# A decoder layer's opening: memory turned raw, memory weights ahead of x, half of x turned among the queries, and the mLSTM pools laid out anew

## The chip, the core and the metric

The kernel runs on one core of a Trainium2 chip. Work is spread over the core's engines, each with its own instruction queue: TensorE (PE, matmuls and transposes, with its weight loads shown as PEld), VectorE (DVE), ScalarE (ACT), GpSimd (POOL), and SyncE (SP), which issues the transfers between HBM and the on-chip memory SBUF. The metric is device microseconds of one execution. The kernel before took 2228.19 us (median of three runs, 2226.64 to 2229.35).

## The reference

One layer over 1024 tokens of width 1024, in float32. What the change touches is the head of the layer and the memory branch, branch C:

```
h = rms_norm(x, norm_mix_g)
proj = h @ w_in                      # the last 512 columns of it are cq
mkv = rms_norm(mem, mem_g) @ w_kv    # 256 memory tokens; 512 key + 1024 value columns
mk = rms_norm(mk per head of 128, k_g);  qh = rms_norm(cq per head of 128, q_g)
p = softmax(qh @ mk.T * 128 ** -0.5);    y_c = p @ mv
gates = sigmoid(h @ w_gate + b_gate)     # 3 x 1024 columns
```

After it come the mLSTM branch, differential attention, three output projections merged by the gates, and an MLP with residuals. The row norm multiplies each row of `mem` by one factor, so it commutes with the matrix product: `(r * mem) @ w = r * (mem @ w)`.

## The kernel before, in words

**Split products.** Every float32 operand of a product is split into a high part (rounded to the matmul type) and a low rest, and a product is three matmuls: high x high, high x low, low x high (`mm3`). A split (`split`, L107) is one ACT instruction for the high part and one DVE instruction for the low part; the low part needs the high part. Operands that must be turned go through a PE transpose into PSUM first; four 128x128 blocks share one PSUM tile, and the splits read it from there. The pool for these tiles, `tp`, has two buffers.

**The opening, `phase_x` with `mem_kv`.** All in one queue order on each engine: two memory tiles (128 tokens x 1024) and the first weights are loaded; each memory tile is squared and summed on ACT (L231), the factor `r` is worked out on POOL (L127, L128), and DVE multiplies the tile by it (L233); then PE turns it (L243) and ACT and DVE split it into `memT` (L114, L115). The key weights `wkv[0]` are loaded in four pieces of 512 KB through a pool of three raw buffers (`rp`) and split (L111, L112). Keys of two token tiles are made one after the other, normed, turned and split into `mkT`. Then the eight tiles of x are loaded; four are normed and turned into the first half of `hT` (`half(0)`), the values from `wkv[1]` follow, `half(1)` does the second half of x, and the values from `wkv[2]` end it. `hT` is the turned, split, normed x that everything later multiplies with.

**Branch C, `branch_c`.** A `stream` of eight query tiles (24 matmuls each, yielding after every three: a position) and then 64 gate positions; `weave` puts other items at positions written out by hand: turn a query tile (`turn`, at 8t + 12), its scores and softmax (`scores`, at 8t + 15, with four exponentials on ACT, L380), the turning of the probabilities (`ptr`) and the products with the values. PE runs this order as written (`pinned`). ACT, DVE, POOL and SP instructions are not pinned: a planner orders them for each engine by readiness and program order, at build time. [...]

**Gates.** `gate_load` loads and splits gate weights in pieces of 256 columns, `gate_steps` runs the gate products; the first two gate groups run at the end of branch C, and each result `gt` is stored through SP (L472).

**The mLSTM branch, `branch_m`.** It begins with eight value tiles `v_tile(3, t)` of 24 matmuls of 264 columns (`wmv`), for which eight weight pieces are loaded into `rp` (three raw buffers) and split into `wp` (25 buffers). Pools are laid out one after the other from the same start as branch C's pools. Before: `gm` (value tiles, gate vectors), `pm3`, `rp`, `wp`, so that the 25 weight buffers lie over what branch C still holds; a buffer can be written once everything that lay on its bytes has been read.

```
gm, pm3, self.rp, self.wp = E2("gm", 1), E2("pm3", 3), E2("rpm", 3), E2("wpm", 25)
```

Of the kernel before, what the change touches and what calls it, by code (L numbers as in the profile page):

```python
# [10 lines left out]
F32 = mybir.dt.float32  # L11
F32R = mybir.dt.float32r
AF = mybir.ActivationFunctionType
# [4 lines left out]
P = 128  # L18
D = 1024
S = 1024  # L20
NT = 8
# [10 lines left out]
def f32(ap):  # L32
    return ap.bitcast(F32)
# [38 lines left out]
class Layer:  # L72
    def __init__(self, tc, a, out):
        self.tc, self.nc, self.a, self.out = tc, tc.nc, a, out
        self.V, self.A = InOrder(tc, tc.nc.vector), tc.nc.scalar
        self.n = 0

# [29 lines left out]
    def split(self, hi, lo, src, scale=None):  # L107

        nc = self.nc
        if scale is None:  # L110
            nc.scalar.copy(hi, src)  # L111
            nc.vector.tensor_sub(lo, src, f32(hi))  # L112
        else:
            nc.scalar.activation(hi, src, AF.Copy, scale=scale)  # L114
            nc.vector.scalar_tensor_tensor(out=lo, in0=src, scalar=scale, in1=f32(hi), op0=ALU.mult, op1=ALU.subtract)  # L115
# [112 lines left out]
    def norm_rows(self, src, r1, scr):  # L228

        nc = self.nc  # L230
        nc.scalar.activation(scr, src, AF.Square, accum_out=r1)  # L231
        self.rsqrt_mean(r1, r1, D, 1)
        nc.vector.tensor_scalar_mul(src, src, r1)  # L233


    def mem_kv(self, pool, tmp, xs):
        nc, a = self.nc, self.a
        memT = tmp.tile([P, NK, 2, 256], F32R, tag="memT", name="memT")
        for k in range(0, NK, 2):
            ps = self.tp_tile()  # L240
            for i in range(2):
                for t in range(2):
                    nc.tensor.transpose(  # L243
                        ps[:, (i * 2 + t) * P : (i * 2 + t + 1) * P], xs[t][:, (k + i) * P : (k + i + 1) * P], self.ident
                    )
# [5 lines left out]
        self.mkT = pool.tile([P, 4, 2, 256], F32R, name="mkT")  # L251
        self.mv = pool.tile([P, 2, 2, D], F32R, name="mv")

        def proj(w, t):
            ps = self.mm_tile()
            for k in range(NK):
                self.mm3(
                    ps, (memT[:, k, 0, t * P : (t + 1) * P], memT[:, k, 1, t * P : (t + 1) * P]), w[k], k == 0, k == NK - 1
                )
            return ps  # L260

        w = self.load_w(a["wkv"][0], 512, 2)
        for t in range(2):
            ps = proj(w, t)
            kr = tmp.tile([P, 512], F32, tag="kr", name=self.name("kr"))
            nc.scalar.copy(kr, ps)
            scr = tmp.tile([P, D], F32, tag="sq", name=self.name("scr"))
            nc.scalar.activation(scr[:, 0:512], ps, AF.Square)
            r4 = tmp.tile([P, 4], F32, tag="r4", name=self.name("r4"))
            nc.vector.tensor_reduce(r4, scr[:, 0:512].rearrange("p (h d) -> p h d", h=4), axis=AX.X, op=ALU.add)  # L270
            self.rsqrt_mean(r4, r4, 128, 4)
            for h in range(4):
                nc.vector.tensor_scalar_mul(kr[:, h * P : (h + 1) * P], kr[:, h * P : (h + 1) * P], r4[:, h : h + 1])
            pt = self.tp_tile()
            for h in range(4):
                nc.tensor.transpose(pt[:, h * P : (h + 1) * P], kr[:, h * P : (h + 1) * P], self.ident)
            p4 = pt.rearrange("p (h t) -> p h t", h=4)
            self.split(self.mkT[:, :, 0, t * P : (t + 1) * P], self.mkT[:, :, 1, t * P : (t + 1) * P], p4)
        for g in range(2):
            w = self.load_w(a["wkv"][1 + g], 512, 2)  # L280
            yield
            for t in range(2):
                ps = proj(w, t)
                s = slice(g * 512, (g + 1) * 512)
                self.split(self.mv[:, t, 0, s], self.mv[:, t, 1, s], ps)

    def phase_x(self, kv, tmp):

        nc, a = self.nc, self.a

        def load(src, tag):
            x = tmp.tile([P, D], F32, tag=tag, name=self.name(tag))
            nc.sync.dma_start(x, src)
            return x

        def norm(x):
            r = tmp.tile([P, 1], F32, tag="r1", name=self.name("r1"))
            scr = tmp.tile([P, D], F32, tag="sq", name=self.name("scr"))
            self.norm_rows(x, r, scr)

        mem = [load(a["mem"][t * P : (t + 1) * P, :], "mx") for t in range(2)]
        for x in mem:
            norm(x)
        gen = self.mem_kv(kv, tmp, mem)
        next(gen)
        xs = [load(a["x"][t * P : (t + 1) * P, :], "xk") for t in range(NT)]

        def half(hf):
            for x in xs[4 * hf : 4 * hf + 4]:
                norm(x)  # L310
            for k in range(NK):
                if k % 2 == 0:
                    sc = self.sc_tile()
                ps = sc[:, k % 2 * 512 : k % 2 * 512 + 512]
                for i in range(4):
                    self.transpose(ps[:, i * P : (i + 1) * P], xs[4 * hf + i][:, k * P : (k + 1) * P])
                s = slice(hf * 512, (hf + 1) * 512)
                self.split(self.hT[:, k, 0, s], self.hT[:, k, 1, s], ps, self.vec[:, R_MIX + k : R_MIX + k + 1])

        half(0)  # L320
        next(gen)
        half(1)
        for _ in gen:
            pass
# [5 lines left out]
    def branch_c(self, pool):  # L330
# [3 lines left out]
        w = self.load_w(a["wcq"], 512, 2)  # L334
        Q, pr, pT = {}, {}, {}

        def stream():
            for t in range(NT):
                ps = self.mm_tile()
                for k in range(NK):  # L340
                    s = slice(t * P, (t + 1) * P)
                    self.mm3(ps, (self.hT[:, k, 0, s], self.hT[:, k, 1, s]), w[k], k == 0, k == NK - 1)
                    if k < NK - 1:
                        yield
# [68 lines left out]

        items = []
# [4 lines left out]
        for hf in range(2):  # L419
            for h in range(4):  # L420
# [4 lines left out]
                add(b + 10, values, hf, h, 1)  # L425
        self.weave(stream(), items)
# [3 lines left out]
    gnext = None  # L430

# [15 lines left out]
    def gate_steps(self, runs):  # L447

        nc = self.nc
        self.gw, self.gate_n = [], 0  # L450
# [1165 lines left out]
    def run(self):  # L1616
        tc, nc = self.tc, self.nc
        with ExitStack() as ctx:
# [22 lines left out]
            with ExitStack() as c1:  # L1641
# [6 lines left out]
                with ExitStack() as c2:  # L1648
                    E2 = lambda *x, **k: c2.enter_context(tc.tile_pool(*x, **k))
                    kv = E2(name="kv", bufs=1)  # L1650
                    self.wp = E2(name="wp", bufs=4)
                    self.rp = E2(name="rp", bufs=3)
                    with tc.tile_pool(name="ptmp", bufs=1) as tmp0, tc.tile_pool(name="ptmp2", bufs=2) as tmp, tc.tile_pool(name="ptmp8", bufs=8) as tmp8:
                        class T:
                            def tile(_, shape, dt, tag, name):
                                p = tmp8 if tag == "xk" else tmp if tag in ("mx", "sq", "r1", "r4") else tmp0
                                return p.tile(shape, dt, tag=tag, name=name)
                        self.phase_x(kv, T())
                    self.gates = self.gate_steps((2, 1, 1, 2, 6))
                    with tc.tile_pool(name="pc", bufs=2) as pc, tc.tile_pool(name="pc1", bufs=1) as pc1, tc.tile_pool(name="pc3", bufs=5) as pc3, tc.tile_pool(name="pc4", bufs=6) as pc4, tc.tile_pool(name="wpc", bufs=8) as self.gwp, tc.tile_pool(name="rpc", bufs=2) as self.grp:  # L1660
# [5 lines left out]
                        self.branch_c(T2())  # L1666
# [104 lines left out]
```

## Time and profile before

| | |
|---|---|
| median of three runs | 2228.19 us |
| the profiled execution, its own time | 2225.85 us |
| its span, first to last instruction | 2224.1 us |
| what lies around the span | 1.75 us |
| PE busy over the span | 2179.7 us, 98% |
| first query tile done | 68.03 us |
| last matmul of branch C done | 199.84 us |

Rows of the timeline give start, duration, engine, line, operation, output and inputs, shape and count, and in brackets how long the engine had been idle and what released it. Rows of the chain of waits give start, duration and what the time went to. Rows of windows give, for a stretch, the busy time and number of instructions of each engine, the clock that PE was granted as a share of full speed, the share of DMA and GB/s. The end of a matmul is modelled and matmuls overlap, so the pace of a row of matmuls is read from the chain of waits, where each piece ends as the next begins.

### The profile page before, as it was taken

To read this page: it belongs to the slowest core of one execution; us is meant where nothing else is said; L and a number is where in the kernel's file an instruction comes from. 1 tells how busy PE (TensorE), PEld (TensorE's weight loads), DVE (VectorE), ACT (ScalarE), POOL (GpSimd) and SP (SyncE) were. 2 spreads that over 40 slices of the span, in tenths; PEclk is the share of its full clock that TensorE was granted. 3 is DMA by queue.
4 is the path that set the end of the run, shared out by engine and by line. 5 is a ranking of instruction groups with operands and counts; after the bars stand their busy time and mean duration, and the time that the engine had idled before them with its cause. 6 is when DMAs were issued, how large, how long until landed. Compare 5 with 4: busy or idle time off the path is not lost.

```text
span 2224.1 us, 30528 instructions
## 1 busy us (share of the span) xinstructions
PE 2179.7 (98%) x11225; PEld 1873.6 (84%) x11225; DVE 1393.2 (63%) x2630; ACT 1011.6 (45%) x1994; POOL 525.5 (24%) x696
## 2 busy tenths in 40 slices
PE   7999999999999999999999999999999999999999
PEld 5878888898899999999888888887887888688887
DVE  6643575564148887888752233453688877767689
ACT  6543355454246666666643121223535444543332
POOL 2100000000011111111000002202566656465553
PEclk9999999999999999999999999999999999999999
DMA  7023122121321100110134344435425444864444
GB/s 249 29 84 112 50 90 82 42 77 38 107 72 34 31 27 26 39 36 29 67 118 139 114 141 134 147 110 198 161 100 196 159 152 152 313 200 144 147 144 169
DMA packets 113612, 247.89 MB, mean 111 GB/s; under 512 B 10897, under 2 KB 19382, under 8 KB 111414
## 3 DMA queue, kind: packets, MB, share of 16 engines
q1 hardware_dynamic: 111158, 233.36, 31.3%
q10 hardware_dynamic: 2304, 12.58, 1.4%
q8 instruction: 88, 1.44, 0.3%
q14 instruction: 62, 0.51, 0.1%
HBM read 178.76 MB, written 67.14 MB: 111 GB/s over the span
## 4 chain that ended last, share of the span: by engine, by line
PE 81%; DVE 7%; DMA 5%; ACT 4%; issue 2%; POOL 1%; SPq 0%; DVEq 0%; ACTq 0%; POOLq 0%
PE mm L91 48%; PE p L91 22%; PE sc L91 6%; PE tp L94 2%; PE po L91 2%; PE pr L94 1%; DMA xr<-h_d 1%; DVE acc L67 1%; DMA raw<-in_wd 1%; DVE w L112 1%; DVE u L67 1%; ACT dpe L1007 1%; DVE wo L67 1%; ACT w L111 0%; DMA wraw<-in_wdown 0%
## 5 line engine op out<-in xcount | busy, mean ns | idle before, releaser
L91 PE MATMUL mm<-w,hT 128*128 128x384 f32 (+3 forms) x2496 | 484.8, 334 | 3.4 <-ACT w L111 2.8
L91 PE MATMUL mm<-hT,w 128*128 128x512 f32 x1920 | 466.5, 395 | 0.1
L91 PEld LDWEIGHTS mm<-hT,w 128*128 128x128 f32 x1920 | 353.2, 188 | 74.3 <-DVE dkl L891 0.4
L91 PEld LDWEIGHTS mm<-w,hT 128*128 128x128 f32 x2496 | 387.9, 190 | 15.9 <-ACT w L111 3.8
L91 PE MATMUL p<-xd,wo 128*128 128x512 f32 x1344 | 310.3, 393 | 5.6 <-DVE c L67 2.2
L91 PE MATMUL p<-xo,wo 128*128 128x512 f32 x1344 | 308.3, 390 | 5.2 <-DVE st L1418 1.8
L91 PEld LDWEIGHTS p<-xd,wo 128*128 128x128 f32 x1344 | 253.6, 189 | 62.2 <-DVE c L67 3.3
L91 PEld LDWEIGHTS p<-xo,wo 128*128 128x128 f32 x1344 | 251.1, 188 | 61.0 <-DVE u L67 3.7
L91 PE MATMUL mm<-kt,w 128*128 128x512 f32 x1152 | 261.6, 389 | 0.0
L112 DVE TENSOR_TENSOR w<-raw,w 128x256 fp32r<-128x256 f32 (+3 forms) x304 | 171.8, 588 | 135.5 <-ACT w L111 134.6
L91 PEld LDWEIGHTS mm<-kt,w 128*128 128x128 f32 x1152 | 216.1, 188 | 45.3 <-DVE w L112 0.5
L111 ACT CAST w<-raw 128x256 fp32r<-128x256 f32 (+3 forms) x304 | 154.5, 530 | 178.3 <-PE mm L91 113.7
L104 ACT CAST wo<-wraw 128x896 fp32r<-128x896 f32 x122 | 114.9, 944 | 212.0 <-PE p L91 109.0
L67 DVE TENSOR_TENSOR wo<-wraw,wo 128x896 fp32r<-128x896 f32 x122 | 144.9, 1205 | 54.2 <-ACT wo L104 54.1
L1145 POOL TENSOR_TENSOR wraw<-wraw 128x128 f32<-128x128 f32 x128 | 93.1, 728 | 248.5 <-DMA wraw<-in_wdown 89.4
L1007 ACT ACTIVATE dpe<-sc,dst,drr 128x256 f32<-128x256 f32 (+7 forms) x128 | 106.7, 834 | 52.5 <-DVE dst L1003 49.2
L999 DVE CUSTOM_DVE_ANT_0 sc<-sc,tmask 128x256 f32<-128x256 f32 (+7 forms) x128 | 97.1, 759 | 22.0 <-PE sc L91 22.0
L127 POOL TENSOR_SCALAR hss<-hss 128x4 f32<-128x4 f32 x8 | 3.3, 408 | 416.2 <-ACT mscr L752 272.9
L1148 POOL TENSOR_TENSOR wraw<-wraw 128x128 f32<-128x128 f32 x128 | 87.1, 680 | 10.0
L1146 POOL TENSOR_TENSOR wraw<-wraw 128x128 f32<-128x128 f32 x128 | 87.3, 682 | 0.0
L1147 POOL TENSOR_TENSOR wraw<-wraw 128x128 f32<-128x128 f32 x128 | 86.4, 675 | 0.0
L127 POOL TENSOR_SCALAR drr<-drr 128x16 f32<-128x16 f32 x16 | 3.6, 223 | 348.2 <-DVE drr L953 331.6
(285 smaller groups left out, 3062.5 us busy)
## 6 DMA issues: line engine op xcount, KB each, us to landing
wraw<-in_wup SPq DMA_DIRECT2D x64, 256.0 KB, 3.4
r_d<-xts SPq DMA_DIRECT2D x16, 1024.0 KB, 4.1
wraw<-in_wdown SPq DMA_DIRECT2D x64, 256.0 KB, 2.9
xd<-r_d SPq DMA_DIRECT2D x19, 768.0 KB, 7.2
xd<-r_d SPq DMA_DIRECT2D x14, 1024.0 KB, 6.6
raw<-in_wgate SPq DMA_DIRECT2D x48, 256.0 KB, 3.1
gates<-gt SPq DMA_DIRECT2D x48, 256.0 KB, 2.0
raw<-in_wd SPq DMA_DIRECT2D x32, 384.0 KB, 3.5
```

The source lines that it names most:

```text
L67: return self.tc.keep_in_program_order(f(*a, **k))
L91: self.pin(self.nc.tensor.matmul(out, l, r, start=start, stop=stop))
L94: self.pin(self.nc.tensor.transpose(out, x, self.ident))
L104: self.A.copy(hi, src)
L111: nc.scalar.copy(hi, src)
L112: nc.vector.tensor_sub(lo, src, f32(hi))
L999: V.tensor_tensor_reduce(out=sc[:, 0:n], in0=sc[:, 0:n], in1=self.tmask[:, D - n : D], scale=1.0, scalar=-3.0e38, op0=ALU.add, op1=ALU.max ...
L1007: nc.scalar.activation(pe[c][:, 0:n], sc[:, 0:n], AF.Exp, bias=t8[:, 2 + c : 3 + c], scale=rr[:, i, c : c + 1], accum_out=t8[:, 4 + c : 5 ...
L1145: G.tensor_add(r[:, 4], r[:, 0], r[:, 3])
L1146: G.tensor_sub(r[:, 5], r[:, 4], r[:, 1])
L1147: G.tensor_sub(r[:, 6], r[:, 1], r[:, 0])
L1148: G.tensor_sub(r[:, 7], r[:, 2], r[:, 5])
```

## The change

Nothing of what is computed changes but the place of the memory norm. The opening is rewritten:

- **Memory turned raw.** Each memory tile is loaded in two halves of columns and turned without the norm; the norm factor `rm` is applied when the keys and values are read out of PSUM.
- **Weights ahead of x.** The raw weights get seven buffers in place of three. All twelve pieces of `wkv` and the four of `wcq` go through them; keys, values 0 and values 1 run one after the other, both token tiles at once per weight piece. Half of x is loaded during values 0 and normed during values 1; its first three blocks are turned before the first query tile, the others inside it.
- **Fixed ACT and DVE order.** In `phase_x` every ACT and DVE instruction of the new code goes through `InOrder`, so that these two engines run the written order as PE does. The same holds for the norms of x's second half and for the first gate weights.
- **x's second half among the queries.** It is loaded into its own pool `px`, normed at positions 12, 15, 18 and 21 of the stream of branch C, and turned at positions 23 to 31. The first eight gate pieces are split at positions 36 to 57.
- **Pools moved.** Branch C's pools now begin with `px` (16 KB per partition), `wp` (32 KB), a spare `gap` (2 KB) and `kv`, with the keys (8 KB) ahead of the values (16 KB). The mLSTM pools begin with `rp` and `wp` (3 + 25 buffers of 2112 bytes, 59136 bytes), ahead of `gm` and `pm3`; they end below the values.

The core of the diff:

```diff
@@ class Layer
+        self.engines = tc.nc.scalar, tc.nc.vector
+        self.ordered = InOrder(tc, tc.nc.scalar), self.V
...
+    def x_turn(self, xs, hf, k):
+        ps = self.tp_tile()
+        for i in range(4):
+            self.transpose(ps[:, i * P : (i + 1) * P], xs[i][:, k * P : (k + 1) * P])
+        s = slice(hf * 512, (hf + 1) * 512)
+        self.split(self.hT[:, k, 0, s], self.hT[:, k, 1, s], ps, self.vec[:, R_MIX + k : R_MIX + k + 1])
...
+    def phase_x(self, kv, tmp, px):
...
+        self.pinned = True
+        A, V = self.engines = self.ordered
...
+        m_load(0)
+        w_raw(0, 0)
+        m_load(1)
+        for q in range(1, 4):
+            w_raw(0, q)
+        w_raw(1, 0)
+        w = [[], [], [], []]
+        mem_turn(0)
+        mem_turn(2)
+        w_split(0, 0, w[0], 2)
+        rm = []
+        ps = [self.mm_tile() for _ in range(2)]
+        for k in range(NK):
+            proj(w[0], ps, k)
+            if k in (0, 2, 4):
+                w_split(0, k // 2 + 1, w[0])
+                w_raw(1, k // 2 + 1)
+            if k in (1, 3):
+                mem_turn(k + 3)
+            if k in (4, 5):
+                r = tmp.tile([P, 1], F32, tag=f"rm{k}", name=self.name("r1"))
+                self.row_scale(mem[k - 4], r, tmp.tile([P, D], F32, tag="sq", name=self.name("scr")))
+                rm.append(r)
+            if k == 5:
+                w_split(1, 0, w[1])
+                w_raw(2, 0)
+        w_split(1, 1, w[1])
+        w_raw(2, 1)
+        kr = [keys(t, ps[t]) for t in range(2)]
...
+        for k in range(NK):
+            proj(w[1], pv, k)
...
+        values(0, 0, pv[0])
+        values(0, 1, pv[1])
+        ps = [self.mm_tile() for _ in range(2)]
+        for k in range(NK):
+            proj(w[2], ps, k)
+            if k in (0, 2):
+                w_split(2, k // 2 + 2, w[2])
+            if k >= 4:
+                self.x_norm(xs[k - 4], tmp, "sq")
+        for t in range(2):
+            values(1, t, ps[t])
+        self.x1 = [x_load(px, 4 + i) for i in range(4)]
+        for k in range(3):
+            self.x_turn(xs, 0, k)
+            if k < 2:
+                w_split(3, k, w[3])
+        wq = w[3]
+        q0 = self.mm_tile()
+        for k in range(NK):
+            self.mm3(q0, (self.hT[:, k, 0, 0:P], self.hT[:, k, 1, 0:P]), wq[k], k == 0, k == NK - 1)
+            if k + 3 < NK:
+                self.x_turn(xs, 0, k + 3)
+            if k in (0, 2):
+                w_split(3, k // 2 + 2, w[3])
+        self.pinned = False
+        self.engines = nc.scalar, nc.vector
+        return wq, q0
@@ branch_c
+        for i in range(4):
+            add(12 + 3 * i, self.x_norm, self.x1[i], pool, "cpe")
+        for k in range(NK):
+            add(23 + 5 * k // 4, self.x_turn, self.x1, 1, k)
+            add(36 + 3 * k, first_gate)
@@ run
+                    px = E2(name="px", bufs=4)
+                    self.wp = E2(name="wp", bufs=4)
+                    gap = E2(name="gap", bufs=1).tile([P, 512], F32, name="gap")
+                    nc.gpsimd.memset(gap[:, 0:1], 0.0)
                     kv = E2(name="kv", bufs=1)
...
-                    gm, pm3, self.rp, self.wp = E2("gm", 1), E2("pm3", 3), E2("rpm", 3), E2("wpm", 25)
+                    self.rp, self.wp, gm, pm3 = E2("rpm", 3), E2("wpm", 25), E2("gm", 1), E2("pm3", 3)
```

`proj` does one weight piece for both token tiles (six matmuls), `keys` reads the keys out of PSUM with the factor `rm`, `values` splits them with it, `row_scale` is the old norm without the multiplication, and `x_norm` is the old norm.

More of the change, by code (lines that the diff above doesn't have):

```diff
@@ L238, in mem_kv, with mem_turn @@
         memT = tmp.tile([P, NK, 2, 256], F32R, tag="memT", name="memT")
-        for k in range(0, NK, 2):
+        self.mkT = kv.tile([P, 4, 2, 256], F32R, name="mkT")
+        self.mv = kv.tile([P, 2, 2, D], F32R, name="mv")
+        def mem_turn(k):
             ps = self.tp_tile()
[L241 to L245, printed above, removed]
+            for t in range(2):
+                for i in range(2):
+                    j = i * 2 + t
+                    self.transpose(ps[:, j * P : (j + 1) * P], mem[t][:, (k + i) * P : (k + i + 1) * P])
@@ L250, in mem_kv, with proj @@
                 )
[L251 to L266, printed above, removed]
+        def proj(w, ps, k):
+            for t in range(2):
+                c = slice(t * P, (t + 1) * P)
+                self.mm3(ps[t], (memT[:, k, 0, c], memT[:, k, 1, c]), w[k], k == 0, k == NK - 1)
```

142 lines of the change are left out of this document (77 added, 65 removed).

## The prediction

> **What bounds the kernel now.** I read the page's head first, then windows cut at the stages that the change touches, then the chain of waits and the timeline inside those with PE idle.
>
> ```profile
> span 2224.1 us, 30528 instructions
> PE 2179.7 (98%) x11225; PEld 1873.6 (84%) x11225; DVE 1393.2 (63%) x2630; ACT 1011.6 (45%) x1994; POOL 525.5 (24%) x696
> ```
>
> PE sets the time: 98% of 2224.1 us. No part of the change removes a matmul, so it can win only idle PE time, or time at a low clock. The windows show where that lies; columns are PE, PEld, DVE, ACT, POOL, clock, DMA share, GB/s.
>
> ```profile
> 0.00:68.00 68.00, 52.98 (x258) 41.52 (x259) 48.94 (x84) 47.52 (x76) 14.59 (x33) 1.00 0.61 212
> 68.00:97.00 29.00, 29.00 (x157) 24.55 (x157) 15.62 (x35) 14.79 (x40) 4.82 (x8) 1.00 0.11 37
> 97.00:146.00 49.00, 45.88 (x245) 37.55 (x244) 24.22 (x49) 22.20 (x56) 4.80 (x8) 1.00 0.17 60
> 146.00:199.00 53.00, 53.00 (x249) 43.39 (x248) 14.92 (x46) 17.12 (x35) 0.00 (x0) 1.00 0.24 85
> 206.00:212.00 6.00, 5.55 (x26) 5.12 (x25) 3.53 (x11) 3.44 (x10) 0.00 (x0) 0.54 0.55 186
> 212.00:230.00 18.00, 18.00 (x150) 18.00 (x149) 8.72 (x34) 7.42 (x22) 0.00 (x0) 1.00 0.30 97
> ```
>
> Three places: the opening to 68 us (15.0 us without PE), 97 to 146 (3.1 us, which no edit addresses), and the seam between branch C and the mLSTM at 200 to 212, with idle time and then a clock of 0.54.
>
> **The seam.** The chain of waits across it:
>
> ```profile
> 197.99 1.84 PE mm L91 x8
> 199.91 0.69 ACT gt L471
> 200.62 1.99 DMA gates<-gt
> 202.71 0.42 ACT w L111
> 203.61 2.60 DMA raw<-in_wmv
> 206.24 0.42 ACT w L111
> 206.70 25.10 PE mm L91 x180
> ```
>
> The last gate matmul ends at 199.84. The gate result must be stored before the weight buffers on its bytes can be written, then the fourth raw piece must be fetched, since only three raw buffers were filled early. At 206.70 the rest begins without another wait: 174 of the 192 value matmuls and six of the next stage. At the pace of the undisturbed window (150 in 18.0 us, 0.120 each) 192 would take 23.0 us and end at 199.8 + 23.0 = 222.8. The trace has the next stage beginning here:
>
> ```profile
> 230.24 1.56 PE L91 MATMUL mm<-hT,w 128*128 128x512 f32 x6
> ```
>
> So the seam costs 230.2 - 222.8 = 7.4 us: about 4 us waiting, the rest at half clock behind it.
>
> The new layout takes that chain away, if the bytes come free as the sizes say: px 16384 + wp 32768 + gap 2048 + keys 8192 = 59392, against 59136 for the mLSTM's raw and weight buffers. They lie on x's second half, the query weights, the spare and the keys, the last of which is read by the scores of the eighth query tile, at about 134 us:
>
> ```profile
> 133.21 1.52 PE L91 MATMUL sc<-mkT,cqT 128*128 128x256 f32 x12
> 133.84 2.43 SPq L592 DMA_DIRECT2D raw<-in_wmv  x3
> 200.49 0.40 ACT L111 CAST w<-raw 128x264 fp32r<-128x264 f32 x1
> ```
>
> Before, three raw pieces are there soon after 134 and are cast only at 200.49. After, the 24 pieces of the first head have some 60 us. They cost ACT 24 x 0.40 = 10 us and DVE about as much, and the window 146 to 199 has 36 us free on ACT and 38 on DVE; 3 MB at the 212 GB/s of the first window take 14 us. This cover is wide. What moves onto the late bytes is `gm` and `pm3`, needed when the first value tile leaves PSUM, 3 us after the seam, and not by a matmul before it. I take the whole **7.4 us**, which is also the most that this place has. The lower bound is 4.0: the casts stay queued behind the last `gt` on ACT, and 8 of 0.42 (3.4) are paid in place of the chain, with no half clock.
>
> **The opening.** Before, the first matmul of the keys starts at 14.82:
>
> ```profile
> 7.03 0.45 PE L192 MATMUL tp<-ident,vraw 128*128 128x128 f32 x1 [7.03 <-DMA vraw<-in_vecs]
> 8.23 1.06 ACT L231 ACTIVATE scr<-mx 128x1024 f32<-128x1024 f32 x1 [2.41 <-DMA mx<-in_mem]
> 11.68 0.75 DVE L233 TENSOR_SCALAR mx<-mx,r 128x1024 f32<-128x1024 f32 x1 [5.48 <-POOL r L128]
> 12.35 0.28 DVE L194 COPY vec<-tp 128x128 f32<-128x128 f32 x1
> 14.82 3.55 PE L91 MATMUL mm<-w,memT 128*128 128x512 f32 x10
> ```
>
> Raw turning drops the square, the power and the multiplication from 8.23 to 12.55 out of this path. The first halves of both tiles are together the 512 KB of the first tile before, so they land near 8.2; 7.8 is a floor, since `vec`, which scales the splits, can be copied at 7.5 at the earliest. Four memory columns are then split on ACT, and half a weight piece:
>
> ```profile
> L114 ACT ACTIVATE memT<-tp,vec 128x256 fp32r<-128x256 f32 x8 | 3.7, 474 | 4.1 <-PE tp L243 2.8 <-DVE memT L115 1.3
> L115 DVE SCALAR_TENSOR_TENSOR hT<-sc,vec,hT 128x512 fp32r<-128x512 f32 x16 | 11.2, 744 | 0.0
> 13.57 1.22 DVE L112 TENSOR_TENSOR w<-raw,w 128x1024 fp32r<-128x1024 f32 x1
> 14.67 1.04 ACT L111 CAST w<-raw 128x1024 fp32r<-128x1024 f32 x1
> 16.33 0.87 DVE L115 SCALAR_TENSOR_TENSOR memT<-tp,vec,memT 128x256 fp32r<-128x256 f32 x2
> ```
>
> ```profile
> 9.19 0.19 ACT L231 ACTIVATION_READ_ACCUMULATOR scr<-mx 128x1 f32 x1
> 11.07 0.58 POOL r L128
> L112 DVE TENSOR_TENSOR mv<-mm,mv 128x512 fp32r<-128x512 f32 x4 | 2.7, 681 | 0.0
> L114 ACT ACTIVATE hT<-sc,vec 128x512 fp32r<-128x512 f32 x16 | 10.3, 695 | 2.5 <-PE sc L94 2.5
> ```
>
> 8.2 + 0.5 (transposes) + 4 x 0.474 + 0.59 = 11.2 for the first matmul. For the pace of PE in steady work, with the whole of a gap-free stretch:
>
> ```profile
> 65.70 5.02 PE mm L91 x22
> 70.72 0.44 PE tp L94 x4
> 73.25 1.42 PE sc L91 x12
> 68.03 0.59 ACT L346 COPY cqr<-mm 128x512 f32<-128x512 f32 x1 [0.40 <-PE mm L91]
> ```
>
> 0.23 us a matmul of 512 columns, 0.11 a transpose, 0.12 a score matmul. The keys, 48 matmuls (11.1) and 8 transposes (0.9), end at 11.2 + 12.0 = 23.2 if nothing is late. I add 1.0 for low parts that come last (pieces of weights and of memory alternate on DVE, 1.22 and 2 x 0.48 for each 2 k against 2.8 on PE), and 0.8 because the first matmuls run slower (the ten from 14.82 take 0.35 each): 25.0. Values 0: 11.1 + 0.9 for the key transposes + 0.5 to wait for its first piece, which stands behind both row squares in ACT's fixed order: 37.5. Values 1: 11.1, to 48.6; the four norms of x fit under it (4 x (1.06 + 0.19) on ACT, 4 x 0.58 on POOL, 4 x 0.75 on DVE).
>
> Behind it DVE sets the pace: 2 value splits of 0.68, 8 turned blocks of 0.744, 4 weight pieces of 1.22 = 12.2, after 0.6 for the first ACT read, and the last three matmuls (0.7): the first query tile ends at 48.6 + 13.5 = 62.1, where PE alone would need 9.1. Before it was 68.0, so it is **5.9 earlier**. But half of x is then still unturned: 32 transposes of 0.11, **3.5 us** of PE, come back inside the queries. DMA doesn't bind: 8 MB of weights, 1 MB of memory and 2 MB of x need 28 us at the 395 GB/s of the fullest stretch, and the last of them are wanted at about 50:
>
> ```profile
> 5.00:10.00 5.00, 0.45 (x1) 0.18 (x1) 0.85 (x5) 1.78 (x4) 0.19 (x1) 1.00 1.03 395
> ```
>
> **x's second half among the queries.** Between positions 23 and 32 PE has 9 x 0.70 + 8 x 0.44 + two score groups of 1.42 + one turn of 0.44, 13.1 us. ACT has 8 splits of 0.70, about one and a half groups of exponentials (the first row below), a query read (1.2, two like the one at 68.03) and a split: 10.8. DVE has 8 x 0.744, a maximum (the second row) and some small ones.
>
> ```profile
> 99.08 2.19 ACT cpe L380 x8
> L375 DVE TENSOR_REDUCE cmx<-sc 128x4 f32<-128x1024 f32 x8 | 9.8, 1225 | 11.6 <-PE sc L91 11.6
> ```
>
> So the sum fits, but a block whose split stands behind a group of exponentials is 2.2 us late, `tp` has two buffers, and a block comes every 1.3 us: one such meeting stalls PE 1 to 2 us. The lower bound is 0 (ACT gets the splits first), the upper bound is every block behind such a group, 8 x (2.2 + 0.7 + 0.74 - 1.3) = 18.7. Only two groups fall in the stretch, so I take **2.0**. Norms at 12 to 21 (5 us of ACT in some 10 of PE) and the gate pieces at 36 to 57, which were split ahead of these positions before, I cost at nothing: 68 to 97 has 14 us of ACT and 13 of DVE free. Without that cover the norms cost up to 2.
>
> The sum: -7.4 - 5.9 + 3.5 + 2.0 = **-7.8 us**, against the profiled execution 2225.85 - 7.8 = 2218.0. The median of the runs is 2.3 above that execution, so for a median I say 2228.2 - 7.8 = **2220.4 us**. All work behind 260 us keeps its order on PE, and PE is its bound, so what is won ahead stays won.
>
> **The rule that speaks against it.** DVE copies `vec` at 12.35, though the transpose that it needs ended at 7.48: it stands behind a multiplication that waits for POOL until 11.68, 4 us of a ready instruction lost. [...]
>
> **The rivals.**
>
> *1. The opening wins more.* If halves land at 7.8 and DVE doesn't bind behind values 1 (its splits are taken while PE still works), the query tile ends nearer 59, and no block meets an exponential: -7.4 - 9 + 3.5 = -12.9, 2215. For it: ACT and DVE each have 20 us free in the old opening. Against: 12.2 us of DVE stand in one row behind the values.
>
> *2. Slower: the turned blocks queue.* From position 23 PE in its fixed order waits for `tp`, and ACT's queue puts exponentials, query reads and gate casts ahead of splits. It decides from 2.3 us a block, all eight: 18.7 in place of 2.0 gives -7.8 + 16.7 = +8.9, 2237. For it: the stretch 97 to 146 already loses 3.1 us to such meetings. Against: only two groups fall among the eight blocks. Half of it gives 2229, no change.
>
> *3. The seam stays half shut.* The planner leaves the casts behind the last gate result, as it did at 200.49: 4.0 in place of 7.4, 2228.2 - 4.4 = 2223.8. For it: the first cast before needed no store and still came after `gt`. Against: its buffer need not have been free earlier.
>
> *4. The change doesn't do what it says.* Late weight pieces hold the fixed order so that the first query tile ends at 68 after all: +5.9, 2226.3.
>
> **How the numbers follow.** Forecast 0.52 (its own range 2217 to 2224), rival 1 0.20, rival 2 0.10, rival 3 0.12, rival 4 0.06. Faster or slower by over 0.2% means below 2223.7 or above 2232.7; within that a measurement of this kernel can't tell it from no change. Faster: 0.9 of the forecast, all of rival 1, a third of rival 3: 0.71. Slower: nearly all of rival 2: 0.09. Same: 0.20. The range 2213 to 2228 leaves out rival 2 and the far edge of rival 1.
>
> **What would show it right or wrong.** The seam: at the end of the second gate group PE goes on without a gap, no clock under 0.9 behind it, casts of `wmv` ahead of the last `gt`, 192 matmuls in 23 us. The opening: first key matmul at 11.2, keys ending at 25, values 0 at 37.5, values 1 at 48.6, the first query read at 62.1, with DVE busy nearly without a gap from 49 to 61. The queries: PE idle at `x_turn` waiting for DVE's or ACT's split, 2 us in all. Wrong would make it: a gap at the seam behind a store or a fetch; a key matmul after 13; stalls of over 5 us ahead of position 40; or gates and mLSTM stages that take longer than before though they are untouched.

## The result: slower by 0.24%

| | before | after |
|---|---|---|
| median of nine runs each | 2228.19 us | 2233.64 us |
| lowest to highest | 2226.64 to 2230.16 | 2230.92 to 2239.01 |
| profiled execution, span | 2224.1 us | 2231.5 us |

The ratio is 1.0024 (95% interval 1.0014 to 1.0035): slower, where 2220.4 was forecast. The page's head of the kernel after:

```profile
span 2231.5 us, 30507 instructions
PE 2182.3 (98%) x11225; PEld 1875.8 (84%) x11225; DVE 1392.1 (62%) x2623; ACT 1011.6 (45%) x1995; POOL 526.8 (24%) x697
```

PE has as many matmuls as before, is 2.6 us busier and 4.8 us more idle. Where, the forecast's own landmarks tell (us from the span's start; the forecast's last two are its 62.1 + 131.8 + 3.5 + 2.0 and 23.0 more):

| | before | forecast | after |
|---|---|---|---|
| first key matmul | 14.82 | 11.2 | 12.79 |
| keys end | | 25.0 | 28.7 |
| values 0 end | | 37.5 | 40.8 |
| values 1 end | | 48.6 | 51.7 |
| first query read | 68.03 | 62.1 | 66.09 |
| last matmul of branch C | 199.84 | 199.4 | 210.9 |
| stage behind the value tiles starts | 230.24 | 222.4 | 236.48 |

Four differences follow. The opening won 1.9 us (forecast 5.9); six more profiles below with the same opening in the same order have the first query read at 63.84 to 66.29. The queries and gates, from the first query read to the last matmul of branch C, went from 131.8 to 144.8: 13.0 lost (forecast 5.5). The seam, from there to the next stage, went from 30.4 to 25.6: 4.8 won (forecast 7.4). Behind it 1.1 more was lost up to 278 us (forecast 0). Together -1.9 + 13.0 - 4.8 + 1.1 = +7.4, as much as lies between the two spans.

**The queries.** Windows of the kernel after in which PE idles or its clock is low, columns as in the prediction:

```profile
75.00:83.00 8.00, 5.41 (x31) 4.23 (x30) 4.52 (x10) 5.56 (x15) 4.16 (x8) 1.00 0.00 0
83.00:87.00 4.00, 4.00 (x18) 3.32 (x17) 2.69 (x4) 2.45 (x6) 0.00 (x0) 0.57 0.00 0
87.00:95.00 8.00, 5.16 (x32) 3.89 (x31) 4.51 (x11) 4.62 (x11) 1.21 (x2) 1.00 0.01 2
110.00:124.00 14.00, 10.48 (x62) 8.15 (x61) 9.38 (x23) 8.33 (x24) 1.73 (x3) 1.00 0.11 39
124.00:128.00 4.00, 4.00 (x13) 3.22 (x14) 1.59 (x3) 0.97 (x2) 0.00 (x0) 0.57 0.20 66
```

PE idles 2.6, 2.8 and 3.5 us in three of them, and in the other two its clock is 0.57: each holds a spell of 3.4 us at half clock. Neither ACT nor DVE is full: they are busy 0.70 of a window at most. PE waits for single instructions that come late. Which ones, PE's waits between 60 and 200 us tell (us in total, times, longest), after:

```profile
PE tp L97 <- DVE hT L118: 2.4, 1, 2.4
PE tp L97 <- DVE cpT L115: 2.0, 2, 1.7
PE sc L94 <- DVE cqT L118: 1.8, 1, 1.8
PE tp L97 <- DVE cqT L118: 1.6, 2, 1.1
PE sc L94 <- ACT cqT L117: 0.8, 1, 0.8
```

and before:

```profile
PE tp L94 <- DVE cpT L112: 1.7, 1, 1.7
PE sc L91 <- ACT cpe L380: 0.6, 1, 0.6
PE tp L94 <- DVE cpe L387: 0.4, 1, 0.4
PE tp L94 <- DVE cqT L115: 0.4, 1, 0.4
```

The whole lists add up to 9.7 from the first query read on, against 3.1. The 6.6 more are a block of x (hT, 2.4), scores that wait for the turned query (sc <- cqT, 1.8 + 0.8), and transposes that wait for a `tp` buffer held by a query or probability split (cqT 1.2 and cpT 0.3 more). The timeline at the scores:

```profile
76.62 1.08 ACT L67 ACTIVATE scr<-xk 128x1024 f32<-128x1024 f32 x1
77.67 1.07 ACT L67 ACTIVATE scr<-xk 128x1024 f32<-128x1024 f32 x1
78.71 0.70 ACT L117 ACTIVATE cqT<-tp,dv 128x512 fp32r<-128x512 f32 x1
...
80.32 0.75 DVE L67 TENSOR_SCALAR xk<-xk,r 128x1024 f32<-128x1024 f32 x1 [0.72 <-POOL r L131]
80.99 0.74 DVE L118 SCALAR_TENSOR_TENSOR cqT<-tp,dv,cqT 128x512 fp32r<-128x512 f32 x1
81.79 1.46 PE L94 MATMUL sc<-mkT,cqT 128*128 128x256 f32 x10 [1.83 <-DVE cqT L118]
...
87.83 0.58 ACT L458 ACTIVATE cpe<-sc,cmx,cr 128x256 f32<-128x256 f32 x1
88.38 1.29 ACT L117 ACTIVATE hT<-tp,vec 128x512 fp32r<-128x512 f32 x2
89.81 1.40 DVE L118 SCALAR_TENSOR_TENSOR hT<-tp,vec,hT 128x512 fp32r<-128x512 f32 x2
90.61 0.66 PE L97 MATMUL tp<-ident,xk 128*128 128x128 f32 x4 [2.35 <-DVE hT L118]
```

The query was turned at 76.6, and its scores are due 2.1 us later, at 78.7. But its high split stands behind two row squares of norms (`xk`) on ACT, and its low split behind a norm's multiplication on DVE, which itself waits for POOL. At 88 it is the meeting that was forecast: two blocks stand behind a group of exponentials.

**The opening.** PE's timeline, after:

```profile
12.79 5.79 PE L94 MATMUL mm<-w,memT 128*128 128x512 f32 x12 [2.66 <-ACT w L67]
18.37 0.65 PE L97 MATMUL tp<-ident,mx 128*128 128x128 f32 x4
18.78 3.01 PE L94 MATMUL mm<-w,memT 128*128 128x512 f32 x12
```

and ACT's beside it:

```profile
11.75 0.47 ACT L67 ACTIVATE memT<-tp,vec 128x256 fp32r<-128x256 f32 x1 [0.58 <-DVE memT L67]
12.12 2.08 ACT L67 CAST w<-raw 128x512 fp32r<-128x512 f32 x3
19.06 0.47 ACT L67 ACTIVATE memT<-tp,vec 128x256 fp32r<-128x256 f32 x1 [4.86 <-PE tp L97]
20.09 0.48 ACT L67 ACTIVATE memT<-tp,vec 128x256 fp32r<-128x256 f32 x1 [0.55 <-DVE memT L67]
20.46 1.04 ACT L67 CAST w<-raw 128x1024 fp32r<-128x1024 f32 x1
```

The first twelve key matmuls take 0.48 us each, the next twelve 0.25; with PE kept busy ahead of them, the first twelve take 3.3 us in place of 5.8 (experiment 10). ACT then idles 4.86 us: its next memory split waits for a transpose behind the slow matmuls, and the weight cast that follows in the written order comes only at 20.46. And ACT's split of the second half of a PSUM tile waits for DVE's of the first half in all four tiles, 0.55 to 0.58 us each. The clock falls to 0.50 in the opening, ahead of the first query read (PE busy, clock, DMA share, GB/s):

```profile
57.00:58.00 1.00, 1.00 (x5) 0.50 0.00 0
58.00:59.00 1.00, 1.00 (x5) 0.50 0.00 0
```

**The seam.** PE's timeline, after:

```profile
210.91 3.09 PE L94 MATMUL mm<-w,hT 128*128 128x264 f32 x24
214.82 3.20 PE L94 MATMUL mm<-w,hT 128*128 128x264 f32 x24 [0.82 <-ACT gt L559]
218.80 17.84 PE L94 MATMUL mm<-w,hT 128*128 128x264 f32 x144 [0.79 <-DVE gf L704]
```

and ACT's:

```profile
212.85 1.33 ACT L114 CAST w<-raw 128x256 fp32r<-128x256 f32 x4 [1.95 <-DMA raw<-in_wmo]
214.09 0.68 ACT L559 ACTIVATE gt<-mm,dv 128x512 f32<-128x512 f32 x1
...
216.99 0.71 ACT L114 CAST w<-raw 128x256 fp32r<-128x256 f32 x2 [1.53 <-DMA raw<-in_wmo]
217.61 0.36 ACT L114 CAST va<-mm 128x256 fp32r<-128x256 f32 x1
```

The chain of store and fetch is gone and no clock is low. But the planner now also hoists casts of weights of later stages (`in_wmqk`, `in_wmo`) ahead of the last gate result and of the first value split. ACT waits there for their fetches, and PE, short of free PSUM tiles, twice waits 0.8 us for what stands behind them.

### The profile page after: what moved, and what is told of

Its sections match the earlier page's. It is cut to its first block, busy times and chain, and to the rows that moved or that the text cites. A ratio compares the mean times of both kernels' runs of the same rounds, so it can differ in the third digit from the quotient of the medians.

```text
span 2231.5 us, 30507 instructions
## 1 busy us (share of the span) xinstructions
PE 2182.3 (98%) x11225; PEld 1875.8 (84%) x11225; DVE 1392.1 (62%) x2623; ACT 1011.6 (45%) x1995; POOL 526.8 (24%) x697
## 4 chain that ended last, share of the span: by engine, by line
PE 77%; DVE 8%; DMA 6%; ACT 5%; issue 2%; POOL 1%; SPq 0%; DVEq 0%; ACTq 0%; POOLq 0%
PE mm L94 44%; PE p L94 22%; PE sc L94 6%; PE tp L97 2%; PE po L94 2%; PE pr L97 1%; DVE acc L67 1%; DVE u L67 1%; DMA kraw<-y 1%; ACT w L114 1%; DMA raw<-in_wd 1%; DMA gl<-in_xT 1%; DVE wo L67 1%; DVE w L115 1%; ACT dpe L1095 1%
## 5 line engine op out<-in xcount | busy, mean ns | idle before, releaser
L115 DVE TENSOR_TENSOR w<-raw,w 128x256 fp32r<-128x256 f32 (+3 forms) x280 | 149.3, 557 | 124.9 <-ACT w L114 123.9
L114 ACT CAST w<-raw 128x256 fp32r<-128x256 f32 (+3 forms) x280 | 134.9, 504 | 178.6 <-PE mm L94 110.6
L1233 POOL TENSOR_TENSOR wraw<-wraw 128x128 f32<-128x128 f32 x128 | 95.6, 747 | 245.4 <-DMA wraw<-in_wdown 99.6
L1236 POOL TENSOR_TENSOR wraw<-wraw 128x128 f32<-128x128 f32 x128 | 87.9, 687 | 9.9
L1235 POOL TENSOR_TENSOR wraw<-wraw 128x128 f32<-128x128 f32 x128 | 88.1, 688 | 0.0
L107 ACT CAST xd<-xd 128x1536 fp32r<-128x1536 f32 (+2 forms) x36 | 54.9, 1528 | 69.0 <-DMA xd<-r_d 68.8
```

Of the source, the lines that this page charges most:

```text
L107: self.A.copy(hi, src)
L114: s.copy(hi, src)
L115: v.tensor_sub(lo, src, f32(hi))
L1233: G.tensor_add(r[:, 4], r[:, 0], r[:, 3])
L1235: G.tensor_sub(r[:, 6], r[:, 1], r[:, 0])
L1236: G.tensor_sub(r[:, 7], r[:, 2], r[:, 5])
```

## Experiments

Each ratio is to runs of the kernel before on the same chip, with its 95% interval. Stage times come from one profiled execution each and are read ahead of 300 us only: behind about 1300 us, profiles of kernels with the same PE order there drift apart by up to 9 us (from the stage behind the value tiles to the end of the span it is 1992.6 us in experiment 9 and 2001.8 in experiment 6). In the cuts of code, `...` stands for what is left out.

**1. The pools alone,** on the kernel before.

```diff
+self.wp, self.rp, gap, kv = ...   # gap 6 KB per partition, kv last
-gm, pm3, self.rp, self.wp = E2("gm", 1), E2("pm3", 3), E2("rpm", 3), E2("wpm", 25)
+self.rp, self.wp, gm, pm3 = E2("rpm", 3), E2("wpm", 25), E2("gm", 1), E2("pm3", 3)
```

> The kernel before with nothing changed but the pools: branch C's weights and raw buffers first, a spare of 6 KB, then keys and values; the mLSTM's raw and weight buffers ahead of gm and pm3. PE's order is the same. Theory (each part of the change has its own price: seam -4.8 us, opening -1.9, queries +13.0, the rest +1): the seam alone is worth 4 to 6 us, 2228.2 - 5 = 2223. Rival (the early casts only move the wait from the seam onto the gate results and value tiles queued behind them on ACT, as two waits of 0.8 us at the seam of the changed kernel hint): no more than 2 us, 2226 or above.

Measured: 0.9974 (0.9964 to 0.9983), median 2221.67. The seam takes 25.1 us in place of 30.4, the queries 131.7 as before. So this part alone wins 5 to 6 us (4 to 8 by the interval), and all the rest of the change together loses: from 0.9974 to 1.0024.

**2. The pools back,** on the kernel after: the old order of `gm`, `pm3`, `rpm`, `wpm`. Branch C's pools keep their new places, so it is not the old layout byte for byte.

> The changed kernel with the mLSTM pools in their old order (gm and pm3 ahead of the raw and weight buffers); all else is kept. Theory: the old wait at the seam returns, +4.8 us, 2233.6 + 4.8 = 2238, with a clock near 0.5 behind it. Rival (the seam closes for another reason, because the whole opening now loads earlier): 2233 to 2235.

Measured: 1.0039 (1.0026 to 1.0052). The seam takes only 26.7 us against 25.6: eight casts of `wmv` stand behind the last gate result again, PE waits 1.1 us ahead of the first value matmul and 1.0 for a fetch later, no store stands in the chain, and no half clock follows. So the old price of 4.8 us does not come back at the seam. The rest of the difference, if it is one (the interval overlaps that of the change), lies behind the stages read. Inconclusive.

**3. x's second half ahead,** normed and turned at the end of the opening, not among the queries.

```diff
+        for x in self.x1:
+            self.x_norm(x, tmp, "sq")
+        for k in range(NK):
+            self.x_turn(self.x1, 1, k)
-            add(12 + 3 * i, self.x_norm, self.x1[i], pool, "cpe")
-            add(23 + 5 * k // 4, self.x_turn, self.x1, 1, k)
```

> The changed kernel with x's second half normed and turned at the end of the opening, ahead of the second query tile, in place of positions 12 to 31. Theory (the turned blocks among the queries cost 13 us where their PE work is 3.5): the queries take 132 us again as before, and the opening pays 4 norms and 8 blocks with little cover, 8 to 9 us, so 2233.6 - 13.0 + 8.5 = 2229. Rival (the stalls belong to the query stream itself, which lost 3 us before too, and would be there without the blocks): the opening pays its 8 and nothing comes back, 2238 or above.

Measured: 1.0048 (1.0035 to 1.006). From the second query read on (73.48 after, 75.42 before, 89.36 here) to the end of branch C it takes 125.5 us, before 124.4 and after 137.4: the loss in the queries goes with x's second half, as the theory said. But ahead of them the work costs more. Two windows of it:

```profile
66.00:89.00 23.00, 16.47 (x72) 12.89 (x73) 10.71 (x15) 9.82 (x17) 4.22 (x9) 0.70 0.14 45
89.00:215.00 126.00, 121.69 (x611) 100.24 (x610) 59.19 (x143) 58.69 (x148) 8.40 (x14) 1.00 0.22 73
```

From the first to the second query read it is 23.1 us where it was 7.4: PE idles 6.5 us of it, and from 69.3 to 83.0 the clock is 0.50 (0.70 as the mean of the window).

**4. Gate pieces free:** the first eight are ordered by the planner.

```diff
-            add(36 + 3 * k, first_gate)
```

> The changed kernel with the first eight gate pieces left to the planner, as before, in place of positions 36 to 57 in fixed order. PE's order is the same. Theory (the fixed place costs about 1 us of late splits at 110 to 124 us and, through the stall there, one stretch at half clock, 1.7): 2230.5 to 2232.5. Rival (the stall at 111 and 121 to 123 us is that of the kernel before, 1.7 us there as here, and the pieces don't matter): 2233 to 2235.

Measured: 1.0033 (1.0021 to 1.0045), queries 144.7. The fixed place of the gate pieces is not the cause.

**5. Free order:** ACT and DVE of the new code are ordered by the planner, all but the multiplications of x's norms on DVE.

```diff
-        self.ordered = InOrder(tc, tc.nc.scalar), self.V
+        self.ordered = tc.nc.scalar, tc.nc.vector
```

> The changed kernel with ACT and DVE instructions of the opening, the norms and the first gate pieces unpinned, so that the planner orders them; PE's order stays. Theory (what waits is PSUM buffers and PE's own order; the fixed order of ACT and DVE is a minor part): within 1.5 us, 2232 to 2235. Rival (the fixed order is the cause: a weight cast that stands behind a memory split, ACT idle for 4.9 us at 14.2, is freed): the keys end 2 to 3 us earlier and the time falls to 2229 or 2230.

Measured: 1.0002 (0.9992 to 1.0011), against 1.0024. The first query read comes at 61.71, near the forecast's 62.1, but as a sum of errors that cancel: first key matmul 13.02 (forecast 11.2), end of values 1 at 50.19 (48.6), then a query tile of 11.5 us (13.5). The keys end 1.2 us earlier than after, the query tile itself takes 2.9 less (0.6 of it because the half clock at 56 us is absent: experiment 2's profile, with the written order and no such spell, has 13.75 for 14.39), the queries take 142.5. The fixed order costs some 5 us in the runs, and the opening has the largest part. The second query tile's scores wait for `cqT` as in the kernel after, 0.7 and 1.8 us: the planner's order puts the squares ahead of its split too.

**6. Spread:** norms at positions 8 to 11, blocks at every second position from 16.

```diff
-            add(12 + 3 * i, self.x_norm, self.x1[i], pool, "cpe")
+            add(8 + i, self.x_norm, self.x1[i], pool, "cpe")
-            add(23 + 5 * k // 4, self.x_turn, self.x1, 1, k)
+            add(16 + 2 * k, self.x_turn, self.x1, 1, k)
```

> The changed kernel with the norms of x's second half at positions 8 to 11 and its blocks turned at every second position from 16 to 30, in place of 12 to 21 and 23 to 31. Nothing is removed. Theory (blocks come faster than ACT and DVE can split them beside a group of exponentials, with two PSUM buffers between, so PE waits for the buffer): with a block every 1.8 us in place of 1.3 the queries take 139 us or less in place of 144.8, and the time falls by 4 to 6 us to 2228 to 2230. Rival (the sum of ACT and DVE work in this stretch is what binds, wherever the blocks stand): 2232 to 2235.

Measured: 1.0021 (1.001 to 1.0032), queries 143.8, where the theory had 139 or less. How dense the blocks stand is not the cause, or not alone.

**7. No norms** for x's second half: the kernel leaves them out and goes on with raw rows, to price them.

```diff
-            add(12 + 3 * i, self.x_norm, self.x1[i], pool, "cpe")
```

> The changed kernel without the four norms of x's second half: tokens 512 to 1023 go on unnormed, all else is kept, PE's order too. It prices the norms. Theory A (turned blocks cost the queries 9.5 us over their PE work, the norms little of it): the wait of 2.6 us for the second query tile's scores at 79 to 82 us goes, 2230 to 2231. Theory B (the norms are the main cost: 5 us on ACT in a queue, each with a power on POOL, make everything behind them late): the queries lose 6 us or more, 2227 or below.

Measured: 1.0013 (1.0004 to 1.0022), queries 141.8, 3.0 less. Both waits of scores for `cqT` (1.8 and 0.8) are gone, the one for a block is 3.1 in place of 2.4, and one half-clock spell remains of two. This is the first theory (2.6 us of waits go), not the second (6 us or more). The blocks keep 141.8 - 131.8 - 3.5 = 6.5 us.

**8. Blocks split by DVE alone,** so that none stands behind ACT's exponentials.

```diff
+            v.tensor_scalar_mul(hi, ps, g)
+            v.scalar_tensor_tensor(out=lo, in0=ps, scalar=g, in1=f32(hi), op0=ALU.mult, op1=ALU.subtract)
```

> The changed kernel with both halves of the split of x's second half on DVE: the high part leaves ACT's queue (8 x 0.70) and goes to DVE's. Theory (a block waits for PSUM because its ACT read stands behind a group of four exponentials, 2.2 us): that wait goes, and with it one stretch at half clock; the queries take 141 to 143 us in place of 144.8, 2230 to 2232. Rival (the sum of what ACT and DVE have to do in the stretch sets it, and DVE now has 5.6 us more): the queries take 145 us or more, 2234 or above.

Measured: 1.0034 (1.0024 to 1.0043), no gain. The profile's queries take 141.6 us, but by the clock: it has no half-clock spell there, and the profiled execution is the fastest of eleven (2230.44; median 2234.57), while the waits from the first query read on add up to 9.2, hardly less than 9.7 after. The exponentials alone are not the cause: DVE, now with both halves, is as late.

**9. The seam's order,** on experiment 1: gate results, value splits and the later weights' casts in the order written.

```diff
-nc.scalar.activation(t, ps, AF.Tanh, ...)
+self.pin(nc.scalar.activation(t, ps, AF.Tanh, ...))
...
+    def split_o(self, hi, lo, src):
+        self.pin(self.nc.scalar.copy(hi, src))
+        self.pin(self.nc.vector.tensor_sub(lo, src, f32(hi)))
```

> The kernel with the pools alone moved (2221.7), and the gate results, the value tiles and the casts of the first query-key and output-gate weights pinned to the written order on ACT and DVE, so that these casts no longer stand ahead of the last gate results. PE's order is the same. Theory (the 25.1 us of the seam with moved pools are 23.0 of matmuls and two waits behind such casts): seam 23.0 to 23.6, 2219.5 to 2220.5. Rival (the waits are fetches that take as long in any order): 2221 to 2223.

Measured: 0.9970 (0.9958 to 0.9982), median 2219.9, the lowest of all kernels here and below both the kernel before and the change. PE's timeline:

```profile
195.80 3.60 PE L91 MATMUL mm<-hT,w 128*128 128x512 f32 x15
199.24 23.63 PE L91 MATMUL mm<-w,hT 128*128 128x264 f32 x192
222.70 1.56 PE L91 MATMUL mm<-hT,w 128*128 128x512 f32 x6
```

All 192 value matmuls run in one piece; the seam takes 23.5 us, the forecast's 23.0. The gain over experiment 1 lies inside the two intervals; the profiles show 1.6 us at the seam.

**10. Warm start,** on the kernel after: 36 transposes of the identity ahead of the first one, 22 behind the first memory blocks.

> The changed kernel with 36 transposes of the identity ahead of the memory and 22 more between its first blocks and the first key matmul, into PSUM that nobody reads: work added, only to keep PE busy. Theory (the first 12 key matmuls take 0.47 us each in place of 0.23 because PE had been idle for 2.7 us and nearly all of the time before; the fixed order passes the 2.5 us on): first 12 matmuls in 3 us, opening 2 to 2.5 us shorter, 2231. Rival (they wait for their operands, and the weight casts behind the memory splits set the end of the keys anyway): no gain, 2233 to 2235.

Measured: 1.0025 (1.0016 to 1.0034). PE's timeline:

```profile
1.51 5.49 PE L97 MATMUL tp<-ident 128*128 128x128 f32 x36 [1.51 <-POOL ident masks.py:199]
...
12.59 0.50 PE L94 MATMUL mm<-w,memT 128*128 128x512 f32 x1 [0.68 <-ACT w L67]
13.32 2.83 PE L94 MATMUL mm<-w,memT 128*128 128x512 f32 x11 [0.22 <-DVE w L67]
```

The first twelve key matmuls take 3.3 us in place of 5.8, and the first query read comes at 63.06, 3.0 earlier (0.8 earlier than in experiment 2's profile). The runs show nothing of it, though with intervals of 0.1% to each side a gain of 3 us would be hard to see; in the profile the queries take 144.9, as after. By the count of PE's matmuls, 2.7 of the 3.0 are still there at 1270 us and gone by 1730, in the stretch where profiles with the same order drift apart. Why is open.

**11. More raw buffers in the old opening,** on experiment 9: five in place of three.

> The kernel with moved pools and pinned seam (2219.9), with five raw buffers of 512 KB in the old opening in place of three, in the room of the spare. Theory (the old opening waits 6.7 us for a weight piece at 25 to 32 us because three buffers hold back its fetch): values 0 start 3 to 5 us earlier, and 2 to 4 us of it reach the first query tile, 2216 to 2218. Rival (more fetches in flight make the first memory tile and the first piece late, and x, which stands behind the weights, delays the blocks as much): 2219 to 2222.

Measured: 0.9979 (0.9971 to 0.9988), first query read at 70.48 in place of 67.41 (the other profiles of the old opening: 68.03 and 68.94). Earlier issue of the weights alone doesn't help the old opening.

**12. Free order with the seam's order:** experiments 5, 4 and 9 together, with the whole new opening.

> The changed kernel in its best form so far: the planner orders ACT and DVE in the opening, the norms and the first gate pieces (2228.3 without more), and the seam is pinned as in the run on the old opening. Theory (the parts add): seam -2, gate pieces 0 to -1, 2225 to 2226.5, still 5 us or more behind the old opening with the same seam. Rival (the stalls among the queries shrink too once gate pieces are free, and the new opening catches up): 2222 or below.

Measured: 0.9990 (0.998 to 0.9999), first query read at 61.42, seam 23.5, queries 142.7. The best form of the change is faster than before, with an interval that ends at 0.9999. Against experiment 9 it is slower, though the two intervals still touch; the stages agree: its opening wins 6.6 us against before (6.0 against experiment 9), and x's second half costs 10.8 in the queries.

## Why the prediction was wrong, step by step

**The step that failed: "x's second half among the queries", "I take 2.0".** Beside the 3.5 us of transposes it cost 13.0 - 3.5 = 9.5 us. The 2.0 was for blocks behind exponentials, and that meeting cost about that: one wait of 2.4. Two things were priced at nothing. "Norms at 12 to 21 ... I cost at nothing: 68 to 97 has 14 us of ACT and 13 of DVE free" counted room, not order: the turned query is wanted 2.1 us after its transposes, and its splits stood behind two squares of 1.07 us on ACT and two multiplications of 0.75 on DVE that wait for POOL (2.6 us of waits, both gone without the norms, experiment 7). The prediction's own sign of being wrong, stalls of over 5 us ahead of position 40, came: 5.4 us. And no term stood for the clock, though the seam before showed a clock of 0.54 behind a gap: each of the two windows with a spell has 4.0 us at a mean clock of 0.57, so 4.0 x 0.43 = 1.7 us lost. The number of spells differs between the profiles, from none to two here; what decides it is not shown (last section). For the profiles of all nine kernels with x's second half in the queries, these are 131.8, plus 3.5 for the transposes, plus the waits of PE from the first query read to 200 us beyond the 3.1 of before, plus 1.7 a spell:

| kernel | waits | spells | by this sum | measured |
|---|---|---|---|---|
| after | 9.7 | 2 | 145.3 | 144.8 |
| pools back (2) | 10.5 | 1 | 144.4 | 144.2 |
| gates free (4) | 9.7 | 2 | 145.3 | 144.7 |
| free order (5) | 8.8 | 1 | 142.7 | 142.5 |
| spread (6) | 9.7 | 1 | 143.6 | 143.8 |
| no norms (7) | 7.7 | 1 | 141.6 | 141.8 |
| blocks on DVE (8) | 9.2 | 0 | 141.4 | 141.6 |
| warm start (10) | 9.8 | 2 | 145.4 | 144.9 |
| free order, seam (12) | 8.9 | 1 | 142.8 | 142.7 |

So the loss is settled as waits and clock, to 0.6 us. Which shortage makes the blocks' share of the waits (two `tp` buffers, or two engines taking turns) is not: experiments 6 and 8 removed one suspected cause each and left the waits, and more buffers weren't tried. The kernel before turned x through `sc` tiles, two blocks in each (`sc<-ident,xk` in its timeline); the change moved the blocks into the two `tp` buffers that queries and probabilities use as well, and what that costs is not shown.

**The second rival was right in part, and held too cheap.** It named a queue ahead of the splits, with PE waiting for `tp`, and a whole price of 18.7; half as much came (9.5), but not all by its way: waits for `tp` beyond those of before make about 4.0 of it, scores that wait for the turned query 2.6, and the low clock, which it did not name, 3.4. "Half of it gives 2229" took no account of the opening and the seam giving less as well. Its bound "against", that only two groups of exponentials fall among the blocks, was true and beside the point, since the norms and the query splits queue too. The written order of ACT and DVE costs some 5 us in the runs (medians 2233.6 after, 2228.3 in experiment 5).

**The opening: right mechanisms, three terms mis-sized.** First key matmul 12.79, not 11.2: the four memory splits on ACT, taken as 4 x 0.474 in one row, run from 9.31 to 12.2, since ACT waits twice among them for DVE's split of the same PSUM tile (0.55 and 0.58 us); that is 1.0 of the 1.6 us. It could have been foreseen: the prediction's row that gave the 0.474 ends with "<-DVE memT L115 1.3", 1.3 us of ACT's idle time in the kernel before. The rest of the 1.6 lies mostly in the transposes ahead of them: they take 0.27 each (eight in 2.18 us), where 0.5 was allowed for all that stand ahead of the first split. The keys took 15.9 us, not 13.8: "0.8 because the first matmuls run slower" was 2.5 (5.8 to 3.3, experiment 10), and the 1.0 for late low parts was 1.2, for memory splits ahead of a cast in the fixed order (experiment 5). Values 0 and values 1 held within half a microsecond. The first query tile took 14.4 in place of 13.5, about 0.6 of it by the half clock at 56 us; with free order, 11.5. The fourth rival's fixed order did hold the opening, at 63.8 to 66.3 in seven profiles where 61.7 and 61.4 were to be had (experiments 5 and 12), but not through late weight pieces: between 8 and 66 us no wait of PE, ACT or DVE ends with a transfer.

**The seam: right mechanism, the size off.** "I take the whole 7.4" was 4.8. Its split, "about 4 us waiting, the rest at half clock", was misread too: before, PE waits 1.13 + 1.25 + 0.45 = 2.8 us there, and the clock is halved from 204.7 to 211.5, which costs 3.4. The chain went, the casts of `wmv` moved ahead, the half clock went. Left over is that early bytes let later casts be hoisted too, and these stand ahead of `gt` and the value splits. Experiment 9 puts them behind and has 23.5 of the forecast 23.0. The third rival expected a half-shut seam, from late casts; it was early ones.

**Behind the seam: "keeps its order on PE, so what is won stays won"** held but for 1.1 us in the stages read. DVE waits for a fetch ahead of the first chunk products, and PE for what follows from it (0.9 more). DVE's timeline, after:

```profile
265.44 0.69 DVE L755 TENSOR_TENSOR wib<-wib,cv 128x512 f32<-128x512 f32 x1 [7.48 <-DMA wib<-g_dwi]
```

It comes 29.0 us behind the start of its stage; before, the same row stands at 256.63, 26.4 us behind it. Why the fetch is later is open.

## What to carry to other kernels

Work moved into a full PE stream is not priced by the free room of the engines that serve it, but by what its instructions stand ahead of: list, for each queue, the result that PE wants next. A gap in that stream can cost more than its length: behind some gaps here the clock fell to 0.50, 1.7 us a spell. When bytes come free earlier, look at everything that the planner can hoist, not only at what was to be hoisted; here the new order of pools was worth 0.26% (0.30% with the order of ACT and DVE at the seam written out), and all else in the change cost 0.5%.

## What the runs showed of the hardware that was not expected

**Half clock behind short gaps.** The spell from 83.3 to 86.7 stands behind waits of 0.76 and 1.83 us, with 0.5 of matmuls between. In the kernel after the clock is 0.50 from 56.02 to 59.43, from 83.32 to 86.74 and from 124.28 to 127.70 us, 3.4 us each; at the seam before it is 0.50 from 204.70 to 211.53, 6.8 us, and in experiment 3 from 69.3 to 83.0, 13.7 us.

How long PE idles ahead does not tell by itself whether a spell comes. In the 3.41 us ahead of the three spells after PE is busy for 1.66, 1.58 and 1.45 us, and for 2.00 ahead of the one at the seam before. But it is also busy for only 1.51 us from 86.74 to 90.15 after, and for 1.71 from 110.00 to 113.40 before, and the clock stays at 1.00 behind both. The same wait, for the split of `cpT`, is 1.69 us at 112.90 before, with no spell behind it, and 1.68 us at 115.19 in experiment 11, with the clock at 0.50 from 115.95 to 119.36. What decides is not shown.

**The clock column is no proof at the start.** Windows of the kernel after (columns as for 57 to 59 us above):

```profile
16.00:17.00 1.00, 1.00 (x4) 1.00 1.02 418
17.00:18.00 1.00, 1.00 (x4) 1.00 1.01 381
18.00:19.00 1.00, 1.00 (x7) 1.00 0.83 315
```

It reads 1.00 throughout, while the number of matmuls a microsecond goes from 4 to 7: the trace has no record of the clock before 18.47 us, so the slow start must be read from the pace. Experiment 10, with PE busy from 1.5 us on, has eleven of the first twelve key matmuls in 2.83 us, 0.26 each.
